# Expert mixtures of a hybrid backbone: gather threaded with the first experts, two more weight buffers, w2 by column halves, paired combines

## The chip, the cores and the metric

One core of a Trainium2 chip runs the whole program. The metric is the time of one execution on the device in microseconds (us); the median of three runs is compared.

## The reference

Four layers work on 256 context and 256 latent tokens of 1024 channels. A layer has a norm, an input projection, three token mixers and an output projection, and then a second norm and a mixture of 16 experts, in which each expert takes the 32 tokens that want it most, separately for context and latent tokens. The change is in the mixture, in the norm at the head of the layer and in the sums of squares between them:

```python
def rmsnorm(x, g):
    y = xf * lax.rsqrt(jnp.mean(xf * xf, axis=-1, keepdims=True) + EPS)
    return (y * g.astype(jnp.float32)).astype(x.dtype)

def modulate(h, shift, scale):
    return h * (1 + scale[:, None]) + shift[:, None]

def moe_ec(h, router_w, w1, w3, w2):
    cap = max(1, CAP_FACTOR * n // N_EXPERTS)          # 32
    probs = jax.nn.softmax((h @ router_w).astype(jnp.float32), axis=-1)
    aff, idx = lax.top_k(jnp.swapaxes(probs, 1, 2), cap)
    xe = h[bidx, idx]
    hid = jax.nn.silu(jnp.einsum('becd,edf->becf', xe, w1)) * jnp.einsum('becd,edf->becf', xe, w3)
    ye = jnp.einsum('becf,efd->becd', hid, w2) * aff[..., None].astype(h.dtype)
    return jnp.zeros_like(h).at[bidx, idx].add(ye)
```

In layers 0 to 2 both streams go through the mixture; in layer 3 only the latent tokens do.

## The kernel before

The residual stream lies transposed in SBUF: `xT` holds 8 blocks of 128 channels by 512 tokens (columns 0 to 255 context, 256 to 511 latent).

**Weights of the experts.** `Weights` (L1474) cuts w1, w3 and w2 of each expert into tiles of 512 KB and loads them, through SP's queue, into a ring of `N_MW` = 22 buffers of the tag `mw`. A pair of experts has 24 tiles in the order w1, w3, w2 (eight each, the two experts in turn), so a mixture has 192. A w1 or w3 tile is 256 input channels by 512 columns (L1490, two runs of 2 KB in each partition), a w2 tile is 128 rows by 1024 columns (L1492, one run of 4 KB). Loads are issued ahead while the output projection runs (`ahead`, two in each of its eight blocks); four of the ring's buffers hold part of that projection's input until its end. After that a load goes out as soon as the tile 22 places before it has been used. SP issues in order.

**Choosing and gathering tokens.** `moe` (L1528) makes the router's softmax, marks the 32 largest of each row with four rounds of max and replace (L1594), numbers the marked tokens by a scan along the row (L1599) and a product (L1601), transposes the numbers (L1604) and compares them with 1 to 32 to get the one-hot matrix `OH` (L1614). The normed tokens are kept as a high and a low part, `tok`. `gather(eh)` (L1622) multiplies them with the one-hot of eight experts, for eight channel blocks `kk` and both streams `s`, and writes `xe`: 16 experts by 64 columns, 32 context tokens and then 32 latent tokens. `gather(0)` stands ahead of all experts, `gather(1)` behind w1 and w3 of pair 0.

**Pairs of experts.** For each of the eight pairs (L1641): w1 and w3 (L1650, the two experts side by side in the array, 64 columns each), the matrix of weights `Ow` and its transpose (L1660 to L1668), the gate (L1670 to L1673), four transposes (L1676), w2 (L1684), whose two column halves are written in turn for each of four row blocks, the scaled outputs as a high and a low part (`yh`, `yl`, L1687, L1688), and the combine (L1694): for each of eight channel blocks two matmuls of 128 x 512 back to token order, added to `xT` by DVE (L1697). The planner of the language orders each engine's instructions by priority and its own estimate of when they are ready; so the trace shows the combine of one pair threaded into w1 of the next.

**Sums and norm.** Behind the last pair, each finished block of `xT` is squared by ACT and summed over its channels by a matmul with ones (`add_all`, L345 to L349): eight in all. Then `rms_scale` (L357) takes the logarithm and the exponential on ACT, and the head of the next layer (L547 to L553) makes the modulated, normed tokens `hh` (high) and `hl` (low) for each of eight blocks: a product on DVE (L549), two scaled shifts on DVE (L552), the high part copied by ACT (L366) and the difference on POOL or DVE in turn (L367). The projection's matmuls (L393) and the small gates (L211) read them.

## Time and profile before

| | us |
|---|---|
| median of 3 runs | 5003.71 (5001.26 to 5008.22) |
| the profiled execution | 5006.14 |
| its span, first to last instruction | 5004.4 |
| PE busy | 4513.4 (90%) |
| DVE busy | 2998.8 (60%) |
| ACT busy | 1470.0 (29%) |
| POOL busy | 1405.1 (28%) |

The mixtures run from about 1027 to 1319, 2296 to 2589, 3573 to 3864 and 4725 to 4988 us of the span; layers 0 to 2 repeat each other closely, so layer 0 stands for them. In the rows below a name such as `L1694` is a line of the kernel before, `out<-in` are the program's tensors (`df`, `dm`, `bi`, `ac`, `ai` are banks of PSUM, `mw` the weight ring), and x counts instructions. fp32 matmuls are two instructions in the trace. PEld is PE's load of the stationary operand. A row of the timeline merges equal instructions that follow one another: its start, the time to the end of the last, and their number. A wait is put down to what came last.

### The profile page before, as it was taken

The numbers are of one execution on the slowest core, as the hardware profiler recorded it, in microseconds if no ns is written. First come the engines' busy times: TensorE is split into PE (matmuls) and PEld (weight loads), VectorE is DVE, ScalarE is ACT, GpSimd is POOL, SyncE is SP. The second block draws the span as 40 slices with busy tenths as digits, with TensorE's granted clock in tenths as the row PEclk, the third lists the DMA queues.
The fourth block names the chain that finished last, engine by engine and source line by source line (L and its number), as shares of the span: only waits on it lengthen the run. The fifth ranks groups of instructions, "written<-read, shape, count | busy, mean of one in ns | idle before, by whom it ended". The sixth has DMA issues, their size and how long they took to land.

```text
span 5004.4 us, 84862 instructions
## 1 busy us (share of the span) xinstructions
PE 4513.4 (90%) x31882; PEld 2934.2 (59%) x31882; DVE 2998.8 (60%) x8123; ACT 1470.0 (29%) x2932; POOL 1405.1 (28%) x1815
## 2 busy tenths in 40 slices
PE   7999999999889999989998999998998888887798
PEld 4666666653466666665336666666633666675533
DVE  4786757533477766663347777656333677776322
ACT  3333323220233332322023333332301433332211
POOL 3332323410243233232014333233300433332400
PEclk9999999999999999999999999999999899898899
DMA  5433446679532434457963244345697233333598
GB/s 219 119 112 110 119 148 202 234 262 393 214 106 65 126 106 125 156 191 257 394 258 110 63 119 112 101 150 167 234 390 289 77 83 84 86 88 107 198 392 315
DMA packets 684010, 886.03 MB, mean 177 GB/s; under 512 B 337072, under 2 KB 361264, under 8 KB 670800
## 3 DMA queue, kind: packets, MB, share of 16 engines
q1 hardware_dynamic: 683600, 880.60, 52.7%
q8 instruction: 252, 4.13, 0.3%
q14 instruction: 158, 1.29, 0.1%
HBM read 795.81 MB, written 84.63 MB: 176 GB/s over the span
## 4 chain that ended last, share of the span: by engine, by line
PE 50%; DVE 20%; DMA 6%; issue 4%; ACT 3%; POOL 2%; SPq 0%; DVEq 0%; ACTq 0%; POOLq 0%
PE df L393 9%; PE dm L393 8%; PE df L1650 5%; PE ai L211 5%; PE bi L211 5%; PE dm L1650 4%; PE bi L1694 3%; PE ac L211 2%; PE ac L1684 2%; PE bi L1684 2%; DMA t<-gates 2%; DVE cv L1037 2%; DMA mw<-in_w_dram 1%; DVE sv L428 1%; POOL wlo L367 1%
## 5 line engine op out<-in xcount | busy, mean ns | idle before, releaser
L367 POOL TENSOR_TENSOR wlo<-wraw,whi 128x512 fp32r<-128x512 f32 x696 | 942.6, 1359 | 1934.3 <-ACT whi L366 1708.0
L393 PE MATMUL df<-big,whi 128*128 128x512 f32 (+1 forms) x2944 | 892.0, 384 | 0.0
L393 PE MATMUL dm<-big,whi 128*128 128x512 f32 (+1 forms) x2368 | 740.1, 392 | 1.1 <-DVE big L367 1.1
L393 PE MATMUL df<-big,wlo 128*128 128x512 f32 (+1 forms) x1536 | 650.8, 424 | 70.3 <-POOL wlo L367 23.2
L366 ACT CAST whi<-wraw 128x512 fp32r<-128x512 f32 x696 | 426.5, 617 | 870.6 <-PE df L393 442.4
L393 PEld LDWEIGHTS df<-big,whi 128*128 128x128 f32 x2944 | 567.5, 201 | 90.8 <-issue 3.7
L393 PE MATMUL dm<-big,wlo 128*128 128x512 f32 (+1 forms) x1248 | 528.5, 424 | 57.0 <-POOL wlo L367 18.6
L393 PEld LDWEIGHTS dm<-big,whi 128*128 128x128 f32 x2368 | 458.9, 198 | 85.4 <-DVE big L367 2.8
L393 PEld LDWEIGHTS df<-big,wlo 128*128 128x128 f32 x1536 | 306.7, 200 | 197.0 <-issue 97.1
L393 PEld LDWEIGHTS dm<-big,wlo 128*128 128x128 f32 x1248 | 247.1, 198 | 164.9 <-issue 71.9
L1650 PE MATMUL df<-mw,big 128*64 128x512 f32 x1024 | 302.2, 610 | 0.0
L1037 DVE SCALAR_TENSOR_TENSOR cv<-cv,par,cv 128x255 f32<-128x255 f32 (+3 forms) x472 | 249.0, 539 | 42.6 <-ACT cv L1034 38.8
L1697 DVE SCALAR_TENSOR_TENSOR big<-bi,der,big 128x256 f32<-128x256 f32 x448 | 191.8, 478 | 120.3 <-PE bi L1694 119.9
L1650 PE MATMUL dm<-mw,big 128*64 128x512 f32 x1024 | 255.7, 594 | 2.1 <-DMA mw<-in_w_dram 1.9
L1657 POOL MEMSET mada<- 128x512 f32 x32 | 16.8, 525 | 800.7 <-PE bi L1694 350.4
L722 DVE SCALAR_TENSOR_TENSOR big<-cv,muc,big 128x252 f32<-128x252 f32 (+2 forms) x280 | 156.6, 581 | 33.2 <-ACT big L719 31.8
L1650 PEld LDWEIGHTS dm<-mw,big 128*64 128x64 f32 x1024 | 80.8, 137 | 152.5 <-issue 136.7
L1688 DVE SCALAR_TENSOR_TENSOR mlof<-ac,aff,mhif 128x512 fp32r<-128x512 f32 x32 | 24.0, 750 | 212.3 <-ACT mhif L1687 212.3
L211 PE MATMUL ai<-AR,BK 64*128 64x128 f32 (+1 forms) x1024 | 124.0, 320 | 29.8 <-POOL BK L905 12.3
L1684 PE MATMUL ac<-mw,mrawf 128*64 128x512 f32 x512 | 139.6, 600 | 9.9 <-ACT mrawf L1678 9.9
L1694 PEld LDWEIGHTS bi<-mada,mhif 128*128 128x128 f32 x256 | 48.0, 187 | 155.1 <-issue 82.7
L1684 PE MATMUL bi<-mw,mrawf 128*64 128x512 f32 x512 | 138.1, 592 | 0.0
(514 smaller groups left out, 7871.8 us busy)
## 6 DMA issues: line engine op xcount, KB each, us to landing
mw<-in_w_dram SPq DMA_DIRECT2D x768, 512.0 KB, 10.4
wraw<-in_w_in_dram SPq DMA_DIRECT2D x536, 256.0 KB, 2.8
adaw<-in_ada_w_dram SPq DMA_DIRECT2D x96, 1024.0 KB, 6.3
gates<-gt SPq DMA_DIRECT2D x114, 256.0 KB, 3.4
wraw<-in_w_branch_dram SPq DMA_DIRECT2D x96, 256.0 KB, 2.7
t<-gates SPq DMA_DIRECT2D x85, 256.0 KB, 3.7
TU<-zoai SPq DMA_DIRECT2D x128, 128.0 KB, 3.1
wraw<-in_w_out_dram SPq DMA_DIRECT2D x64, 256.0 KB, 5.1
```

What stands on the lines that cost most here:

```text
L211: mm(o, a, b, **kw)
L366: se.copy(dst_hi, src)
L367: eng.tensor_tensor(dst_lo, src, dst_hi.bitcast(F32), ALU.subtract)
L393: mm(ps[:, c0:c1], a[:, k % 4, :], bk[:, c0:c1], start=(n == 0), stop=(n == 3 * nk - 1))
L428: ve.tensor_tensor(tv, Xb[:, j + 1:, j:j + 1].to_broadcast(sh), Xb[:, j:j + 1, 0:j].to_broadcast(sh), ALU.mult)
L722: ve.scalar_tensor_tensor(dst, src, muc[:, 1 + q, rb:rb + 1], dst, ALU.mult, ALU.add)
L1037: ve.scalar_tensor_tensor(dst, src, cw[:, cb, t:t + 1], dst, ALU.mult, ALU.add)
L1650: mm(ps[64 * q:64 * q + 64, :], xe[k // 4][:, k % 4, e0 + q, :], wt[q][:, k2 * 512:(k2 + 1) * 512], start=(k == 0), stop=(k == 7))
L1684: mm(py[hf][64 * q:64 * q + 64, :], hT[:, kk, 64 * q:64 * q + 64], wt[q][:, hf * 512:(hf + 1) * 512], start=(kk == 0), stop=(kk == 3))
L1688: ve.scalar_tensor_tensor(yl[hf], py[hf], aff, yh[hf].bitcast(F32), ALU.mult, ALU.subtract)
L1694: mm(pcb[:, n], y[db // 4][:, db % 4 * 128:(db % 4 + 1) * 128], Cm[:, n], start=y is yh, stop=y is yl)
L1697: ve.scalar_tensor_tensor(xT[:, db, cs_], pcb[:, cs_], der[:, 3, db, s:s + 1], xT[:, db, cs_], ALU.mult, ALU.add)
```

## The change

- The ring grows from 22 to 24 buffers (`N_MW`), the cap on loads ahead from 18 to 20 (`N_PRE`; the eight blocks call for 16). Some small tiles of the routing share buffers.
- A w2 tile is now 256 rows by 512 columns, so w2 is multiplied one column half after the other.
- The slots come from a product with a triangular matrix (three small matmuls) in place of scan and product.
- `gather` takes a list of channel blocks. Two blocks are gathered ahead of the experts, then two more ahead of each of the first three steps of pair 0's w1. In every second pair of experts context and latent columns change places.
- Pairs 0 to 5 are combined two by two: the outputs of four experts are masked and added so that one tile holds the context tokens of four experts and another the latent tokens; 32 matmuls of 256 columns then serve two pairs, where 32 of 512 did. Pairs 6 and 7 are combined as before.
- The sums of squares: the squares of blocks 0+1, 2+3 and 4+5 are added on POOL, so five matmuls with ones in place of eight. A dummy logarithm behind the last pair's transposes loads ACT's table early.
- The norm at the layer's head: DVE multiplies by scale and by r in one instruction for each stream, ACT adds the shift while it writes the high part; the low part comes from one DVE instruction per stream (odd blocks) or from another ACT shift and a POOL difference (even blocks).

The diff, cut to its core:

```diff
...
-N_MW = 22
+N_MW = 24
...
-N_PRE = 18
+N_PRE = 20
...
+        def add_two(self, k, x, ps):
+            sq = self.z.mt([512], *(("ys", 2) if k in (1, 3, 5) else ("t2",)))
+            se.activation(sq[:, self.n], x[:, self.n], AF.Square)
+            if k == 0:
+                self.held, self.sent = [], 0
+            if k < 6 and k % 2 == 0:
+                self.first = sq
+            elif k < 6:
+                gp.tensor_tensor(self.first[:, self.n], self.first[:, self.n], sq[:, self.n], ALU.add)
+                self.held.append(self.first)
+            else:
+                self.held.append(sq)
+            while self.held and (k == 7 or k % 2 == 0 and k > 2 and len(self.held) > 1):
+                mm(ps[:, self.n], C["ones"], self.held.pop(0)[:, self.n], start=(self.sent == 0), stop=(self.sent == 4))
+                self.sent += 1
...
                     t = zr.mt([512], "t2")
-                    ve.tensor_tensor(t, xT[:, k, :], r, ALU.mult)
-                    for s in range(2):
-                        ts_ = t[:, s * 256:(s + 1) * 256]
-                        ve.tensor_scalar(ts_, ts_, der[:, 0, k, s:s + 1], mod[:, k, s:s + 1], ALU.mult, ALU.add)
-                    split(hh[:, k, :], hl[:, k, :], t, (gp, ve)[k % 2])
+                    cs_ = [slice(s * 256, s * 256 + 256) for s in range(2)]
+                    for s, c in enumerate(cs_):
+                        ve.scalar_tensor_tensor(t[:, c], xT[:, k, c], der[:, 0, k, s:s + 1], r[:, c], ALU.mult, ALU.mult)
+                    for s, c in enumerate(cs_):
+                        se.activation(hh[:, k, c], t[:, c], AF.Identity, bias=mod[:, k, s:s + 1])
+                    if k % 2:
+                        for s, c in enumerate(cs_):
+                            ve.scalar_tensor_tensor(hl[:, k, c], t[:, c], mod[:, k, s:s + 1], hh[:, k, c].bitcast(F32), ALU.add, ALU.subtract)
+                    else:
+                        for s, c in enumerate(cs_):
+                            se.activation(t[:, c], t[:, c], AF.Identity, bias=mod[:, k, s:s + 1])
+                        gp.tensor_tensor(hl[:, k, :], t, hh[:, k, :].bitcast(F32), ALU.subtract)
...
             else:
-                sy.dma_start(t, A["w2"][l, e, (j - 8) * 128:(j - 7) * 128, :])
+                hf, j = (j - 8) // 2, j % 2
+                src = A["w2"][l, e, j * 256:(j + 1) * 256, hf * 512:(hf + 1) * 512].rearrange("(k p) f -> p k f", p=128)
+                sy.dma_start(t.rearrange("p (k f) -> p k f", k=2), src)
...
-        sel, slot = z.mt([256], "sel"), z.mt([256], "slot")
-        ve.tensor_scalar(sel[lp], wk[lp], -1.0, None, ALU.is_equal)
-        ve.tensor_tensor_scan(slot[lp], C["ones"][lp, 0:1].to_broadcast([64 - 32 * st0, 256]), sel[lp], 0.0, ALU.mult, ALU.add)
-        ve.tensor_tensor(slot[lp], slot[lp], sel[lp], ALU.mult)
+        ve.tensor_scalar(wk[lp], wk[lp], -1.0, None, ALU.is_equal)
         pst = z.psm()
         for q in range(2):
-            te.transpose(pst[:, 64 * q + 32 * st0:64 * q + 64], slot[lp, q * 128:(q + 1) * 128], ident[lp, lp])
-        stm = z.mt([2, 64], "stm")
+            te.transpose(pst[:, 64 * q + 32 * st0:64 * q + 64], wk[lp, q * 128:(q + 1) * 128], ident[lp, lp])
         sv = slice(32 * st0, 64)
-        ve.tensor_copy(stm[:, :, sv], pst[:, 0:128].rearrange("p (q e) -> p q e", q=2)[:, :, sv])
+        sel, stm = z.mt([2, 64], "sel"), z.mt([2, 64], "stm")
+        ve.tensor_copy(sel[:, :, sv], pst[:, 0:128].rearrange("p (q e) -> p q e", q=2)[:, :, sv])
+        pst = z.psm()
+        mm(pst[:, 32 * st0:64], C["mf_0"], sel[:, 0, sv], start=True, stop=True)
+        mm(pst[:, 64 + 32 * st0:128], C["ones"], sel[:, 0, sv], start=True, stop=False)
+        mm(pst[:, 64 + 32 * st0:128], C["mf_0"], sel[:, 1, sv], start=False, stop=True)
+        ve.tensor_tensor(stm[:, :, sv], pst[:, 0:128].rearrange("p (q e) -> p q e", q=2)[:, :, sv], sel[:, :, sv], ALU.mult)
...
+        def gather(eh, kks):
+            for kk in kks:
...
-                    o, pv = xe[g][:, k, 8 * eh:8 * eh + 8, 32 * s:32 * s + 32], ps.rearrange("p (e c) -> p e c", e=8)
+                    xv = xe[g][:, k, 8 * eh:8 * eh + 8, :].rearrange("p (a r q) c -> p a r q c", r=2, q=2)
+                    pv = ps.rearrange("p (a r q c) -> p a r q c", a=2, r=2, q=2)
                     sc, sh = der[:, 1, kk, s:s + 1], mod[:, 24 + kk, s:s + 1]
-                    if s:
-                        se.activation(o, pv, AF.Identity, scale=sc, bias=sh)
-                    else:
-                        ve.tensor_scalar(o, pv, sc, sh, ALU.mult, ALU.add)
-        gather(0)
+                    for r_ in range(2):
+                        o = xv[:, :, r_, :, 32 * (s ^ r_):32 * (s ^ r_) + 32]
+                        if s:
+                            se.activation(o, pv[:, :, r_], AF.Identity, scale=sc, bias=sh)
+                        else:
+                            ve.tensor_scalar(o, pv[:, :, r_], sc, sh, ALU.mult, ALU.add)
+        gather(0, range(2))
...
             for wn in ("w1", "w3"):
                 ps = psd()
                 for kk in range(4):
+                    if pr_ == 0 and wn == "w1" and kk < 3:
+                        gather(0, range(2 * kk + 2, 2 * kk + 4))
                     wt = [W.take() for q in range(2)]
...
                 ab.append(ps)
             if pr_ == 0:
-                gather(1)
...
+                gather(1, range(8))
+            if pr_ < 6 and pr_ % 2 == 0:
...
+                aff, af = z.mt([2], "aff"), z.mt([2, 2], "af", 2)
+                ve.tensor_scalar(Cm[:, n], pc[:, n], 0.0, None, ALU.is_gt)
+                ve.tensor_reduce(aff[:, st0:], pc[:, n].rearrange("p (s w) -> p s w", w=256), AX.X, ALU.add)
+                for r_ in range(2):
+                    for s in range(st0, 2):
+                        ve.tensor_tensor(af[:, r_, s:s + 1], aff[:, s:s + 1], C["qd"][:, r_ ^ s:(r_ ^ s) + 1], ALU.mult)
...
+            if pr_ == 7:
+                se.activation(z.mt([1], "lnt"), hT[:, 0, 0:1], AF.Ln, scale=0.0, bias=C["eps"])
             py = [psum("ac"), psum("bi")]
-            for kk in range(4):
-                wt = [W.take() for q in range(2)]
+            for hf in range(2):
+                for kk in range(4):
+                    if kk % 2 == 0:
+                        wt = [W.take() for q in range(2)]
+                    for q in range(2):
+                        mm(py[hf][64 * q:64 * q + 64, :], hT[:, kk, 64 * q:64 * q + 64], wt[q][:, kk % 2 * 512:kk % 2 * 512 + 512], start=(kk == 0), stop=(kk == 3))
+            r_ = pr_ % 2
+            if pr_ >= 6:
+                yh, yl = [w2k("hif", F32R) for _ in range(2)], [w2k("lof", F32R) for _ in range(2)]
                 for hf in range(2):
-                    for q in range(2):
...
-            yh, yl = [w2k("hif", F32R) for _ in range(2)], [w2k("lof", F32R) for _ in range(2)]
+                    se.activation(yh[hf], py[hf], AF.Copy, scale=aff[:, 0:1])
+                    ve.scalar_tensor_tensor(yl[hf], py[hf], aff[:, 0:1], yh[hf].bitcast(F32), ALU.mult, ALU.subtract)
+                if pr_ == 7:
+                    X["ss"] = psum("dm")
+                for db in range(8):
+                    pcb = psum("bi")
...
+                    if pr_ == 7:
+                        sums.add_two(db, xT[:, db], X["ss"])
+                continue
+            if r_ == 0:
+                ys = [[w2k("rawm") for hf in range(2)], [z.mt([512], "ys", 2) for hf in range(2)]]
...
             for hf in range(2):
-                se.activation(yh[hf], py[hf], AF.Copy, scale=aff)
-                ve.scalar_tensor_tensor(yl[hf], py[hf], aff, yh[hf].bitcast(F32), ALU.mult, ALU.subtract)
-            if pr_ == 7:
-                X["ss"] = psum("dm")
+                for s in range(st0, 2):
+                    if r_ == 0:
+                        se.activation(ys[s][hf], py[hf], AF.Copy, scale=af[:, 0, s:s + 1])
+                    else:
+                        ve.scalar_tensor_tensor(ys[s][hf], py[hf], af[:, 1, s:s + 1], ys[s][hf], ALU.mult, ALU.add)
+            if r_ == 0:
+                continue
+            yh, yl = [[[w2k(x + f, F32R) for _ in range(2)] for f in "fm"] for x in ("hi", "lo")]
+            for hf in range(2):
+                for s in range(st0, 2):
+                    split(yh[s][hf], yl[s][hf], ys[s][hf], (ve, gp)[hf])
             for db in range(8):
                 pcb = psum("bi")
-                for y in (yh, yl):
-                    mm(pcb[:, n], y[db // 4][:, db % 4 * 128:(db % 4 + 1) * 128], Cm[:, n], start=y is yh, stop=y is yl)
+                for s in range(st0, 2):
+                    cs_ = slice(s * 256, (s + 1) * 256)
+                    for y in (yh, yl):
+                        mm(pcb[:, cs_], y[s][db // 4][:, db % 4 * 128:(db % 4 + 1) * 128], Cm[:, cs_], start=y is yh, stop=y is yl)
                 for s in range(st0, 2):
                     cs_ = slice(s * 256, (s + 1) * 256)
                     ve.scalar_tensor_tensor(xT[:, db, cs_], pcb[:, cs_], der[:, 3, db, s:s + 1], xT[:, db, cs_], ALU.mult, ALU.add)
...
```

## Rows read from the trace of the kernel before

**Rows 1.** Stretches: length, busy (count) PE, PEld, DVE, ACT, POOL; clock, DMA share, GB/s

```profile
1044.80:1056.10 11.30, 11.23 (x66) 9.80 (x66) 6.34 (x16) 3.95 (x7) 0.00 (x0) 0.76 0.00 0
1178.70:1210.40 31.70, 29.88 (x120) 10.54 (x120) 11.44 (x26) 2.49 (x6) 0.53 (x1) 1.00 1.04 394
1304.70:1321.30 16.60, 14.47 (x40) 5.85 (x40) 8.18 (x19) 9.64 (x15) 5.08 (x4) 1.00 0.32 91
1327.40:1345.00 17.60, 17.53 (x67) 9.03 (x68) 11.29 (x21) 5.54 (x9) 8.34 (x6) 0.83 0.39 149
4850.00:4950.00 100.00, 93.13 (x396) 34.87 (x393) 24.59 (x52) 9.42 (x15) 1.58 (x3) 1.00 1.04 393
```

**Rows 2.** Waits of weight loads, 1130-1290, then 4800-4972: us, times, longest

```profile
PEld df L1650 <- DMA mw<-in_w_dram: 0.4, 1, 0.4
...
PEld dm L1650 <- DMA mw<-in_w_dram: 13.5, 20, 1.2
```

**Rows 3.** PE in order of time, layer 0: start, us, instruction, count, idle

```profile
1056.14 7.09 PE L1650 MATMUL df<-mw,big 128*64 128x512 f32 x32
...
1178.77 0.49 PE L1694 MATMUL bi<-mada,mhif 128*128 128x512 f32 x1 [0.81 <-ACT mhif L1687]
...
1192.97 7.45 PE L1650 MATMUL dm<-mw,big 128*64 128x512 f32 x31
...
1210.44 0.50 PE L1694 MATMUL bi<-mada,mhif 128*128 128x512 f32 x1 [0.76 <-ACT mhif L1687]
...
1303.62 1.08 PE L1684 MATMUL bi<-mw,mrawf 128*64 128x512 f32 x4
```

**Rows 4.** Loads issued by SP in order of time, layer 0

```profile
1058.10 0.80 SPq L1492 DMA_DIRECT2D mw<-in_w_dram  x2
...
1282.10 1.62 SPq L374 DMA_DIRECT2D wraw<-in_w_in_dram  x2
```

**Rows 5.** DMA issues of the page: count, KB each, median us to landing

```profile
mw<-in_w_dram SPq DMA_DIRECT2D x768, 512.0 KB, 10.4
...
t<-gates SPq DMA_DIRECT2D x85, 256.0 KB, 3.7
...
t<-gates SPq DMA_DIRECT2D x23, 128.0 KB, 2.9
```

**Rows 6.** Loads issued by SP in order of time, last layer

```profile
4841.88 9.40 SPq L1490 DMA_DIRECT2D mw<-in_w_dram  x8
...
4852.20 9.91 SPq L1490 DMA_DIRECT2D mw<-in_w_dram  x8
...
4863.02 9.79 SPq L1492 DMA_DIRECT2D mw<-in_w_dram  x8
```

**Rows 7.** All engines in order of time, layer 0, choosing tokens

```profile
1040.43 1.63 DVE L1599 TENSOR_TENSOR_SCAN slot<-cst,sel 64x256 f32<-64x256 f32 x1
...
1042.10 1.30 DVE L1601 TENSOR_TENSOR slot<-slot,sel 64x256 f32<-64x256 f32 x1
...
1044.87 0.58 PE L1630 MATMUL bi<-OH,mhim 128*128 128x256 f32 x1 [0.94 <-DVE OH L1614]
```

**Rows 8.** Waits of SP, 1056 to 1090: us in total, times, longest

```profile
SPq L1490 <- PE df L1650: 10.5, 5, 7.6
```

**Rows 9.** Groups by line in the tail: count, busy us, mean ns, idle before

```profile
L349 PE MATMUL dm<-t,cst 128*128 128x512 f32 x16 | 8.0, 612 | 0.7 <-ACT t L348 0.7
L1697 DVE SCALAR_TENSOR_TENSOR big<-bi,der,big 128x256 f32<-128x256 f32 x16 | 6.8, 478 | 5.7 <-PE bi L1694 5.7
...
L1694 PE MATMUL bi<-mada,mhif 128*128 128x512 f32 x8 | 4.4, 544 | 1.1 <-ACT mhif L1687 0.8 <-DVE big L1697 0.2 <-DVE mlof L1688 0.2
...
L1694 PEld LDWEIGHTS bi<-mada,mlof 128*128 128x128 f32 x8 | 1.5, 188 | 1.2 <-DVE mlof L1688 0.6 <-issue 0.5
```

**Rows 10.** Groups by line in the first norm of layer 1

```profile
L552 DVE TENSOR_SCALAR t<-t,der,mod 128x256 f32<-128x256 f32 x16 | 5.5, 407 | 0.0
L549 DVE TENSOR_TENSOR t<-big,adm 128x512 f32<-128x512 f32 x8 | 5.4, 689 | 5.2 <-POOL big L367 3.5 <-ACT adm L362 1.6
```

More of the change, by code (lines that the diff above doesn't have):

```diff
@@ L1590, in moe @@
                 tok[g, t] = (hi, lo)
[L1591 removed]
+        wk, m8 = z.mt([256], "lT"), z.mt([8], "m8")
         src = pp[:, 0:256]
@@ L1619, in moe @@
             for xg in xe:
-                gp.memset(xg[:, :, :, 0:32], 0.0)
-        def gather(eh):
-            for kk in range(8):
+                for r_ in range(2):
+                    gp.memset(xg.rearrange("p k (a r q) c -> p k a r q c", r=2, q=2)[:, :, :, r_, :, 32 * r_:32 * r_ + 32], 0.0)
+        def gather(eh, kks):
+            for kk in kks:
                 g, k = kk // 4, kk % 4
@@ L1665, in moe @@
-            Cm = w2k("ada", F32R)
-            aff = z.mt([1], "aff", 2)
-            ve.tensor_scalar(Cm[:, n], pc[:, n], 0.0, None, ALU.is_gt)
-            ve.tensor_reduce(aff, pc[:, n], AX.X, ALU.add)
+                gather(1, range(8))
+            if pr_ < 6 and pr_ % 2 == 0:
+                Ow = w2k("ada").rearrange("p (t q r c) -> p t q r c", t=4, q=2, r=2)
+                for t in range(tl, 4):
+                    s = t // 2
+                    ov = OHf[:, t, e0 * 32:e0 * 32 + 128].rearrange("p (r q c) -> p r q c", r=2, q=2)
+                    av = lg[:, t, e0:e0 + 4].rearrange("p (r q) -> p r q", r=2)
+                    for r_ in range(2):
+                        ve.tensor_tensor(Ow[:, t, :, r_ ^ s], ov[:, r_], av[:, r_, :, None].to_broadcast([128, 2, 32]), ALU.mult)
+                pc = z.psm()
+                for t in range(tl, 4):
+                    te.transpose(pc[:, t * 128:(t + 1) * 128], Ow[:, t].rearrange("p q r c -> p (q r c)"), ident)
+                Cm = w2k("ada", F32R)
+                aff, af = z.mt([2], "aff"), z.mt([2, 2], "af", 2)
+                ve.tensor_scalar(Cm[:, n], pc[:, n], 0.0, None, ALU.is_gt)
+                ve.tensor_reduce(aff[:, st0:], pc[:, n].rearrange("p (s w) -> p s w", w=256), AX.X, ALU.add)
+                for r_ in range(2):
+                    for s in range(st0, 2):
+                        ve.tensor_tensor(af[:, r_, s:s + 1], aff[:, s:s + 1], C["qd"][:, r_ ^ s:(r_ ^ s) + 1], ALU.mult)
+            elif pr_ >= 6:
+                Ow = w2k("ada").rearrange("p (t e c) -> p t e c", t=4, e=2)
+                gp.memset(Ow, 0.0)
+                for t in range(tl, 4):
+                    o = 32 * ((t // 2) ^ (pr_ % 2))
+                    ve.tensor_tensor(Ow[:, t, :, o:o + 32], OHf[:, t, e0 * 32:e0 * 32 + 64].rearrange("p (e c) -> p e c", e=2),
+                                     lg[:, t, e0:e0 + 2, None].to_broadcast([128, 2, 32]), ALU.mult)
+                pc = z.psm()
+                for t in range(tl, 4):
+                    te.transpose(pc[:, t * 128:(t + 1) * 128], Ow[:, t].rearrange("p e c -> p (e c)"), ident)
+                Cm = w2k("ada", F32R)
+                aff = z.mt([2], "aff")
+                ve.tensor_scalar(Cm[:, n], pc[:, n], 0.0, None, ALU.is_gt)
+                ve.tensor_reduce(aff[:, 0:1], pc[:, n], AX.X, ALU.add)
```

19 lines of the change are left out of this document (6 added, 13 removed).

## The prediction

> **What bounds the kernel now.** I read the table of stretches first, for the share of the DMA engines and of PE in each stage of an expert mixture. In layer 0 the gather of the tokens (1044.8 to 1056.1) has a DMA share of 0.00: all weight buffers are full and none is free yet. A pair of experts in the middle (1178.7 to 1210.4) has PE busy for 29.88 of 31.7 us and a DMA share of 1.04 at 394 GB/s: both are at their limit. The tail behind the last w2 (1304.7 to 1321.3) has 0.32 again, and the last layer's middle (4850 to 4950) 1.04 with PE at 93 of 100 [rows 1]. Then the waits of PE's weight loads tell which of the two is late: from 1130 to 1290 they waited 0.4 us for a weight tile, in the last layer 13.5 us in 20 waits, at a granted clock of 1.00 [rows 1, 2]. So layers 0 to 2 are set by PE, with the DMA less than 1% behind it, and layer 3 by the DMA.
>
> PE's order in time gives the prices: a pair takes 1210.44 - 1178.77 = 31.67 us; its w1 stage, into which the combine of the pair before is threaded, 1192.97 - 1178.77 = 14.2, while pair 0's w1, with no combine, took 7.09. The last w2 of layer 0 ends at 1303.62 + 1.08 = 1304.7 [rows 3]. In the DMA queue in order of time the first load into a freed buffer goes out at 1058.10, and the first load for the next layer, right behind the last w2 load, at 1282.10 [rows 4]; with 10.4 us to landing [rows 5] the last w2 tile is there at about 1282.1 - 1.3 + 10.4 = 1291.2. PE then ends w2 13.5 us behind the stream. That lag is what the change can win at most if the stream stays as it is.
>
> **The speed of the stream.** In the last layer eight loads are under way at a time (10.4 us to landing are eight times 1.3), so an issue goes out when the load eight places before it lands. The first eight issues of a pair, paced by landings of w2 tiles, take 4852.20 - 4841.88 = 10.32 us, 1.29 each; the next eight, paced by w1 tiles, 4863.02 - 4852.20 = 10.82, 1.35 each [rows 6]. All are 512 KB; a w2 tile is read as rows of 4 KB, the others as rows of 2 KB. The change reads w2 as half rows of 2 KB, so I price it like w1: 0.06 more for each of the 56 w2 tiles behind the first pair, 3.4 us per layer. The Trainium skill, "DMA: Bandwidth & Descriptors", section Specifications, has a DMA at line rate from 512 B up, by which the halves would cost nothing; the rows disagree by 0.06 us, and by the page the sum would be 13.6 us better (a rival below).
>
> **Layers 0 to 2, to the end of w2.** The scan (1.63) and the product (1.30) of the slots go from DVE's chain; three small matmuls and a product read from PSUM come in. From the scan's start to the first gather matmul there are 1044.87 - 1040.43 = 4.4 us [rows 7]; of these 2.9 go, and about 1.3 come (my estimate: the transposes, the copy and the handing over that stand behind the product now take 4.4 - 2.9 = 1.5 together with the one-hot; between 0.5 and 2), so the gather starts 1.6 earlier. Experts inside the gather: the first slots come free some 6 us earlier, but PE has the same gathers, w1 and w3 to do before it reaches pair 0's w2. The queue runs dry there already today: its longest wait for a free slot is 7.6 us [rows 8], which ends only when w2 frees slots. With two more buffers it is tile 40 of 192 instead of tile 38 that waits for the first w2 slot. So the lead of the stream is 1.6 + 2 x 1.29 = 4.2, less 3.4 for the half rows: 0.8 us, and the last tile lands at 1290.4. Its matmuls are a quarter of a stage, 7.09 / 4 = 1.8 us [rows 3]: end of w2 at 1292.2 by the DMA.
>
> By PE alone: combines threaded into a w1 go from seven to four (pairs 0+1, 2+3, 4+5, then 6), so 3 x 7.1 = 21.3 us go, and 1.6 from the start: 1281.8. A combine of four experts has the same columns in twice as many matmuls; between nothing and 16 more weight loads of 0.19 [rows 9] each, 3.0, three times: 1281.8 to 1290.8. More DVE and ACT work comes (masking, four evictions and four splits every second pair), off the path: in a pair DVE was busy 11.44 and ACT 2.49 of 31.7 [rows 1]. So PE ends before the DMA either way, and the stream sets the end: 1304.7 - 1292.2 = 12.5 gained. Next late is the DMA, in all four layers.
>
> **The tail.** PE is busy 14.47 of 16.6 us from 1304.7 on [rows 1]; 8.0 of it are the sums of squares, eight of two matmuls each, of which five stay: 3.0 gone. PE waits 1.1 for the first evictions [rows 9]; with w2 by halves of its columns the first half is evicted under the second: that goes too. The POOL adds (three of about 1.3, like the four that make up POOL's 5.08 of 16.6 [rows 1]) go under POOL's idle time, and the last two squares need none. Bounds: 2, if the order of PE's queue stays as poor, to 7, where DVE's 16 updates (6.8) [rows 9] with a square and two sums after them are all that is left. I take 4.1. The early load of the logarithm's table is worth nothing here: today's load lies beside the last sums.
>
> **The first norm.** DVE's part falls from 8 x 0.689 + 16 x 0.407 plus the four differences to 24 pieces of about 0.48; ACT gets 24 half pieces for 8 whole ones [rows 9, 10]. DVE's stage would be a third shorter. But from 1327.4 to 1345 PE is busy 17.53 of 17.6 us, at clock 0.83 [rows 1]: it is fed fast enough. Only the first piece comes sooner: 0.69 + 2 x 0.41 and ACT's copy become two halves of 0.48 with ACT's first half under DVE's second, about 0.7 less; with a little of the slow clock, 1. Bounds -1 (ACT late) to 4.
>
> **Sum.** Layers 0 to 2: 3 x (12.5 + 4.1 + 1) = 52.8. Last layer: already paced by the DMA, so its lead of 0.8, and 3 in its tail (sums of half the width, 1.3; evictions 1.1; some of the table load, which is not covered there): 3.8. First norm of layer 0: 1. Together 57.6 us. The profiled execution took 5006.1 (span 5004.4), 2.4 over the median of 5003.7: 5006.1 - 57.6 = 4948.5, or 4946 beside the median.
>
> **Rivals.** *Half rows cost nothing* (they read like 4 KB rows): 3.4 more in each layer, 4932. For it: neighbouring halves are read soon after each other. Against: w1's price. 12%. By the page named above this would be the case. *PE stays the bound*: the wide combine, its splits or the two banks it shares keep PE near its old pace, and w2 ends only 4 us sooner: 3 x (4 + 4.1 + 1) + 4.8 = 32, 4972. For it: twice as many matmuls, and four evictions and four splits that must end before the first of them. 17%. *The order doesn't come as written* (the planner that orders PE's queue keeps the gather whole and the tail as it is): the DMA limit barely moves, the tail gives 2, 3 x (12 + 2) + 3 = 45, 4959. 15%. *The tail and the norm give all they can*: 3 x (12.5 + 7 + 4) + 6 = 76, 4928. 8%. *Slower*: half rows in steps of 4 KB may read worse than whole rows of 2 KB. The nearest rows are the loads of the gates: halves of rows, 128 KB, took 2.9 us where whole rows, 256 KB, took 3.7 [rows 5], 1.57 times the time per byte, though much of that is latency. At 1.29 x 1.57 = 2.03 us a tile the 224 w2 tiles of four layers cost 0.68 x 224 = 152 more: 5098. It turns the result from 1.35 + 57.6 / 224 = 1.61 us a tile on. 8%. *No change*, by smaller losses of the same kind: 4%.
>
> **How the numbers follow.** The forecast has 36%: 4946. Two in ten may be left out: the slower case with no change, and the outer ends of the fast one; the range goes from 4908 (the two fast rivals together, and a little) to 4986 (PE the bound with a tail of nothing). Faster by over 0.2%, about what a measurement of this kernel can tell from no change, holds the forecast and four rivals: 0.88; same 0.04; slower 0.08.
>
> **What would show it.** Right: in layers 0 to 2 PE's loads wait for weight tiles as in the last layer now; 24 loads take 32.4 us instead of 31.9; the last w2 matmuls end 2 us behind the last landing; DMA share stays over 1 to the end. Wrong: w2 tiles that land at 1.29, or above 1.6; PE still without waits for tiles in pairs 5 to 7; a clock below 1.00 between pairs; a tail of 16 us.

## The result and the profile after

The changed kernel takes 4942.2 us (median of four runs, 4935.1 to 4953.0) beside 5005.8 us (5001.3 to 5008.2): a ratio of 0.9876, 95% interval 0.9855 to 0.9897. The forecast was 4946. The profiled execution took 4935.1 us, its span 4933.3, so 71.1 us less than the span of before, of which some 7 are this execution's own (4942.2 - 4935.1).

The total came out as forecast, its parts did not. I measure with two marks in each layer: the start of the softmax's reduction to the maximum on DVE, and the end of the last update of xT behind the mixture. From the first to the second (a mixture) before took 286.0, 287.8, 285.3 and 259.5 us in the four layers, after 276.0, 275.2, 275.3 and 260.8: 31.3 us less where the sum of the prediction had 53.6, and the last layer longer. The stretches between the mixtures are 39.4 us shorter in these two executions, where it had 4 (the first norm).

The stretches of the changed kernel, as in [rows 1] (length; busy us and count of PE, PEld, DVE, ACT, POOL; clock, DMA share, GB/s): pair 5 of layer 0, the tail from the end of w2 to the norm's first product, the first norm of layer 1, the middle of the last layer. Pairs are counted from 0.

```profile
1184.70:1217.20 32.50, 28.52 (x103) 8.75 (x101) 5.46 (x9) 3.68 (x6) 0.00 (x0) 1.00 1.05 387
1288.10:1302.80 14.70, 11.43 (x28) 3.77 (x27) 6.52 (x23) 8.35 (x14) 6.68 (x6) 0.88 0.53 198
1302.80:1318.50 15.70, 11.78 (x43) 4.24 (x44) 13.30 (x24) 10.02 (x24) 5.39 (x4) 0.78 0.40 138
4780.00:4880.00 100.00, 89.78 (x347) 29.38 (x345) 17.57 (x36) 7.46 (x12) 3.59 (x4) 1.00 1.05 387
```

The loads that SP issues, layer 0 and then the last layer, in order of time (start, us of the group, engine, line, count); L1519 loads w2, L1515 w1 and w3:

```profile
1195.02 9.86 SPq L1519 DMA_DIRECT2D mw<-in_w_dram  x8
1205.86 20.72 SPq L1515 DMA_DIRECT2D mw<-in_w_dram  x16
1227.55 9.81 SPq L1519 DMA_DIRECT2D mw<-in_w_dram  x8
1238.35 21.00 SPq L1515 DMA_DIRECT2D mw<-in_w_dram  x16
1260.18 10.00 SPq L1519 DMA_DIRECT2D mw<-in_w_dram  x8
...
4855.27 9.94 SPq L1519 DMA_DIRECT2D mw<-in_w_dram  x8
4866.09 20.79 SPq L1515 DMA_DIRECT2D mw<-in_w_dram  x16
```

In layer 0 the queue now keeps the even step that only the last layer had in [rows 6]: 24 loads take 1227.55 - 1195.02 = 32.5 us. The sixteen issues from 4866.09 on are paced by eight landings of w2 and eight of w1, 1.35 us each (the next w2 load goes out at 4887.75); the w2 step was 1.29 in [rows 6]. The rate is 387 GB/s for 394.

What PE's weight loads waited for from 1100 to 1290 us (us in total, times, longest), which was 0.4 us for weight tiles in [rows 2]:

```profile
PEld dm L1686 <- DMA mw<-in_w_dram: 5.8, 8, 1.2
PEld df L1686 <- DMA mw<-in_w_dram: 5.4, 8, 1.2
```

Of these 11.2 us, 10.6 lie in w1 and w3 of pair 5 (1184.7 to 1206.4); behind them PE waits for no tile. The last w2 load went out at 1269.66; with 10.8 us to landing it is there at 1280.5. PE in order of time shows that w2 ended at 1286.00 + 1.93 = 1287.9, 7.4 us behind it. Between its matmuls (L1745) stands the combine (L1757).

```profile
1276.05 3.65 PE L1745 MATMUL ac<-mw,mrawf 128*64 128x512 f32 x16 [0.67 <-ACT mrawf L1735]
1279.54 1.02 PE L1745 MATMUL bi<-mw,mrawf 128*64 128x512 f32 x2
1280.49 0.50 PE L1757 MATMUL bi<-mada,mhif 128*128 128x512 f32 x1
1281.28 0.50 PE L1757 MATMUL bi<-mada,mlof 128*128 128x512 f32 x1 [0.28 <-DVE mlof L1751]
1281.71 1.93 PE L1745 MATMUL bi<-mw,mrawf 128*64 128x512 f32 x6
...
1286.00 1.93 PE L1745 MATMUL bi<-mw,mrawf 128*64 128x512 f32 x6
```

So two questions went to the chip: which edit shortened the stretches between the mixtures, and why PE is late again at the end of a mixture that the stream sets in its middle.

### The profile page after: what moved, and what is told of

The parts are those of the page before. It is cut to its first block, busy times and chain, and to the rows that moved or that the text cites. A ratio compares the mean times of both kernels' runs of the same rounds, so it can differ in the third digit from the quotient of the medians.

```text
span 4933.3 us, 84704 instructions
## 1 busy us (share of the span) xinstructions
PE 4447.4 (90%) x31792; PEld 2903.0 (59%) x31792; DVE 2927.6 (59%) x8016; ACT 1526.7 (31%) x3100; POOL 1416.8 (29%) x1826
## 3 DMA queue, kind: packets, MB, share of 16 engines
q14 instruction: 158, 1.29, 0.1%
## 5 line engine op out<-in xcount | busy, mean ns | idle before, releaser
L411 PE MATMUL df<-big,whi 128*128 128x512 f32 (+1 forms) x2944 | 884.8, 382 | 0.0
L411 PE MATMUL dm<-big,whi 128*128 128x512 f32 (+1 forms) x2368 | 735.3, 390 | 0.0
L411 PE MATMUL df<-big,wlo 128*128 128x512 f32 (+1 forms) x1536 | 645.9, 420 | 65.9 <-ACT gt L590 21.4
L411 PEld LDWEIGHTS df<-big,whi 128*128 128x128 f32 x2944 | 562.4, 199 | 89.8 <-issue 3.8
L411 PE MATMUL dm<-big,wlo 128*128 128x512 f32 (+1 forms) x1248 | 524.8, 421 | 60.2 <-POOL wlo L385 17.4
L411 PEld LDWEIGHTS dm<-big,whi 128*128 128x128 f32 x2368 | 456.3, 197 | 80.1 <-issue 1.6
L411 PEld LDWEIGHTS df<-big,wlo 128*128 128x128 f32 x1536 | 303.9, 198 | 188.1 <-issue 102.0
L411 PEld LDWEIGHTS dm<-big,wlo 128*128 128x128 f32 x1248 | 245.5, 197 | 163.3 <-issue 57.6
L1686 PE MATMUL df<-mw,big 128*64 128x512 f32 x1024 | 282.8, 604 | 3.7 <-DMA mw<-in_w_dram 3.6
L1728 DVE SCALAR_TENSOR_TENSOR t<-t,df 128x512 f32<-128x512 f32 x32 | 22.0, 687 | 274.1 <-ACT t L1727 274.1
L385 POOL TENSOR_TENSOR mlof<-mrawm,mhif 128x512 fp32r<-128x512 f32 x9 | 11.6, 1284 | 540.3 <-ACT mhif L384 540.3
L1745 PE MATMUL bi<-mw,mrawf 128*64 128x512 f32 x512 | 154.5, 601 | 0.3 <-DMA mw<-in_w_dram 0.3
L1686 PEld LDWEIGHTS df<-mw,big 128*64 128x64 f32 x1024 | 73.3, 136 | 131.4 <-issue 96.1
L1730 DVE TENSOR_TENSOR t<-t,dm 128x512 f32<-128x512 f32 x32 | 22.0, 687 | 193.6 <-PE dm L1686 193.6
L212 PEld LDWEIGHTS ai<-AR,BK 64*128 64x128 f32 x1024 | 91.2, 201 | 72.3 <-issue 30.3
## 6 DMA issues: line engine op xcount, KB each, us to landing
mw<-in_w_dram SPq DMA_DIRECT2D x768, 512.0 KB, 10.8
```

The costliest lines, as they stand in the source:

```text
L212: mm(o, a, b, **kw)
L385: eng.tensor_tensor(dst_lo, src, dst_hi.bitcast(F32), ALU.subtract)
L411: mm(ps[:, c0:c1], a[:, k % 4, :], bk[:, c0:c1], start=(n == 0), stop=(n == 3 * nk - 1))
L1686: mm(ps[64 * q:64 * q + 64, :], xe[k // 4][:, k % 4, e0 + q, :], wt[q][:, k2 * 512:(k2 + 1) * 512], start=(k == 0), stop=(k == 7))
L1728: ve.scalar_tensor_tensor(th, th, 1.0, ab[0], ALU.add, ALU.mult)
L1730: ve.tensor_tensor(hid, th, ab[1], ALU.mult)
```

## The experiments

All twelve runs in one table. "Mixtures" is the sum over the four layers as above, to the last update; "to the norm" adds the time from the last update to the first product of the next norm, for three layers (4.8 us each before); "norm" is the sum over the layers from that product to the end of the norm's 32-matmul product (tile bi<-big,TU); "rest" is the sum from there to the next softmax. The last four columns are one profiled execution, in us; the ratio is to the kernel before on the same chip.

| kernel | median | ratio, 95% interval | mixtures | to the norm | norm | rest |
|---|---|---|---|---|---|---|
| before | 5005.8 | 1 | 1118.6 | 1133.0 | 83.7 | 3725.4 |
| after | 4942.2 | 0.9876 (0.9855-0.9897) | 1087.3 | 1101.7 | 65.9 | 3705.2 |
| n1, before with the new norm | 4984.2 | 0.9954 (0.9936-0.9972) | 1118.9 | 1133.3 | 64.1 | 3726.3 |
| n2, after with the old norm | 4974.5 | 0.9945 (0.9926-0.9965) | 1086.1 | 1100.5 | 87.8 | 3718.7 |
| n3, after, w2 by 4 KB rows | 4938.8 | 0.9876 (0.9856-0.9897) | 1078.5 | 1092.8 | 65.9 | 3718.5 |
| n4, before, w2 by half rows | 5006.5 | 1.0008 (0.9998-1.0018) | 1125.0 | 1139.3 | 83.7 | 3721.4 |
| n5, after with 22 buffers | 4951.3 | 0.9905 (0.9878-0.9931) | 1095.2 | 1109.6 | 65.8 | 3702.5 |
| n6, after, gather first | 4940.1 | 0.9880 (0.9855-0.9906) | 1084.8 | 1099.2 | 65.9 | 3713.4 |
| n7, after, unpaired | 4993.8 | 0.9995 (0.9980-1.0009) | 1130.3 | 1146.5 | 64.2 | 3733.6 |
| n8, after with the scan | 4951.1 | 0.9902 (0.9881-0.9924) | 1084.8 | 1099.2 | 65.9 | 3733.0 |
| n9, after with eight sums | 4954.3 | 0.9910 (0.9889-0.9931) | 1086.6 | 1102.8 | 63.2 | 3724.5 |
| n10, halves in pair 7 alone | 4922.2 | 0.9846 (0.9820-0.9871) | 1064.9 | 1079.2 | 65.9 | 3713.3 |
| n11, no halves | 4929.6 | 0.9854 (0.9833-0.9874) | 1057.3 | 1079.8 | 64.3 | 3727.8 |
| n12, banks exchanged | 4958.2 | 0.9919 (0.9899-0.9939) | 1083.8 | 1104.9 | 64.2 | 3736.4 |

The rest is code that no edit touches, and it goes from 3702 to 3736 us. Two things go with that. One is the granted clock: the four kernels whose profiled execution had a mean clock of 0.946 or 0.948 (n12, before, n7, n11) took 3725 to 3736 us, the three with 0.954 (after, n2, n5) 3702 to 3719. The other is the order in which the planner set this code. In layers 1 and 2 DVE's instructions stand in nearly one order in before, n1, n4 and n12, in another in n7 and n11, and in a third in after and the other seven; the rest of these two layers takes 1920 to 1933 us in the first order, 1921 and 1935 in the second, 1909 to 1922 in the third. What the clock and what the order is worth no run separates. The mixtures, whose pairs of experts run at a clock of 1.00, repeat to 1 or 2 us in a layer, so edits are read from the columns of the stages, and the medians only have to agree.

### The first norm

n1 puts the hunk of the norm into the kernel before, n2 takes it out of the changed one:

```diff
-    ve.tensor_tensor(t, xT[:, k, :], r, ALU.mult)
-    ... scale and shift of both halves on VectorE, then split
+    ve.scalar_tensor_tensor(t[:, c], xT[:, k, c], der[...], r[:, c], ALU.mult, ALU.mult)
+    se.activation(hh[:, k, c], t[:, c], AF.Identity, bias=mod[:, k, s:s + 1])
...
```

Expected of n1:

> The kernel before with the new first norm alone. The prediction (PE is fed fast enough, only the first piece counts) expects 1 us per layer, 4 us: 5002 us beside 5006. The theory from the two traces: the stretches from the last update of a mixture to the next mixture together were 39.3 us shorter after the change (11.1, 7.1, 11.5 and 9.6 us), and the norm is the only edit in them, so the norm alone brings 39 us: 4967 us. Rival: only the norm's own stage is shorter by its cause (about 4 us in a layer, 16 us) and the rest of the 39 us is another order of the queues that came with the other edits: 4990 us.

Expected of n2:

> The changed kernel with the old first norm. By the prediction 4 us are lost: 4946 us. By the theory from the traces 39 us are lost: 4981 us, and the stretches between the mixtures are as long as before. By the rival some 16 us are lost: 4958 us.

n1 brought 19 us in the medians (by its ratio 23, interval 14 to 32), n2 lost 32. In the stages the norm took 22.3, 19.8, 19.8 and 21.8 us before and 15.8, 15.8, 15.8 and 16.6 in n1: 19.6 us, and nothing else moved (mixtures 1118.9, rest 3726.3). n2 differs from after by 21.9 us in the norm and 13.5 in the rest. So the rival holds: about 20 us are the norm's, five in a layer; of the 39.4 us between the two first profiles some 18 are the norm, 20.2 the rest (3725.4 - 3705.2). Of these 20.2, 12.3 lie in layers 1 and 2, whose order changed, and the order came with the other edits, as the rival has it: n1 keeps that of before, n2 that of after. What the 20.2 us owe to the order and what to chance stays open; eight kernels of one order spread from 3702 to 3733 us.

Why the norm could gain, the trace shows. PE of the kernel before in layer 1 in order of time (L393 is the projection w_in, L211 the product with TU), then DVE's last difference there:

```profile
1333.02 2.16 PE L211 MATMUL bi<-big,TU 128*32 128x512 f32 x16
1335.11 0.50 PE L393 MATMUL dm<-big,wlo 128*128 128x512 f32 x1
...
1341.34 0.62 PE L393 MATMUL df<-big,whi 128*128 128x512 f32 x2
...
1342.59 1.27 PE L211 MATMUL bi<-big,TU 128*32 128x512 f32 x8
```

```profile
1341.52 1.24 DVE L367 TENSOR_TENSOR big<-t,big 128x512 fp32r<-128x512 f32 x1 [0.69 <-ACT big L366]
```

The same of the changed kernel:

```profile
1308.76 4.79 PE L212 MATMUL bi<-big,TU 128*32 128x512 f32 x22
1314.37 2.57 PE L212 MATMUL bi<-big,TU 128*32 128x512 f32 x8 [0.82 <-DVE big L574]
...
1318.46 1.04 PE L212 MATMUL bi<-big,TU 128*32 128x512 f32 x2
```

PE was busy all the time before, but with w_in matmuls that stood ready (L393, 31 of them between DVE's first product and the end of the TU product); the eight matmuls that close that product start at 1342.59, as DVE's last difference ends (1342.76). With the new norm 13 of the ready matmuls fall into the stretch (L411), and the product ends at 1319.5, 16.7 us behind the first piece for 19.8. The busy share by itself shows little: of the 3.9 us that PE is idle in the 15.7 above, 3.1 lie ahead of its first norm matmul, at 1305.90. In n1 the last two matmuls of the product wait for DVE's last difference:

```profile
1330.81 1.04 PE L211 MATMUL bi<-big,TU 128*32 128x512 f32 x2 [0.64 <-DVE big L556]
```

### What half rows cost

n3 gives the changed kernel whole rows, n4 the kernel before half rows; the matmuls and the code's order stay, so in both w2 is multiplied with parts of the tiles that are not meant for it. The edit of n3:

```diff
-    src = A["w2"][l, e, j * 256:(j + 1) * 256, hf * 512:(hf + 1) * 512].rearrange("(k p) f -> p k f", p=128)
-    sy.dma_start(t.rearrange("p (k f) -> p k f", k=2), src)
+    sy.dma_start(t, A["w2"][l, e, (j - 8) * 128:(j - 7) * 128, :])
```

Expected of n3:

> The changed kernel, with each w2 tile loaded as 128 whole rows of 4 KB instead of 256 half rows of 2 KB, everything else as it is (the halves of the tiles are then not the weights that the matmuls want: w2 is computed with others). In the trace after the change a tile of half rows took 1.353 us, in the trace of before a tile of whole rows 1.282 us: 0.07 a tile, 4 us for 56 tiles. The prediction, in which the stream sets the end of all four mixtures, expects 13.6 to 16 us: about 4927 us. The theory from the traces: in layers 0 to 2 PE ends w2 8 us behind the last landing without having waited for its tiles, so the stream is worth less than 1 us there and only the last layer gains its 4 to 5 us: about 4936 us. If half rows cost nothing by themselves and the later landings have another cause: 4942 us.

Expected of n4:

> The kernel before, with each w2 tile loaded as 256 half rows of 2 KB, everything else as it is (the matmuls of w2 so use other weights). By the prediction's price of 0.06 us a tile the stream is 3.4 us longer in a layer. In layers 0 to 2 PE is 13.5 us behind the stream and hides it, the last layer shows it: 3.4 to 4 us, 5010 us. If PE's lag hides nothing, because each pair waits for its own tiles, 14 to 16 us: 5021 us. If half rows cost nothing: 5006 us.

n3's mixtures are 1.4, 2.1, 1.3 and 4.0 us shorter than after's: only the last layer is set by the stream to its end. n4's are 1.3, -0.3, 1.0 and 4.4 us longer than before's: PE's lag of 13.5 us hides the price in three layers. Both last layers fit the price of 0.07 us a tile (56 tiles, 3.9 us), and n3 speaks against a stream that sets the end of all four mixtures after the change.

### Buffers and gather

n5 sets `N_MW = 22`, `N_PRE = 18`; n6 has `gather(0, range(8))` ahead of the experts and none inside w1.

Expected of n5:

> The changed kernel with 22 buffers (18 loaded ahead) instead of 24 (20). By the prediction the stream sets the end of all four mixtures and two tiles of lead are 2 x 1.29 = 2.6 us in each: 10 us lost, 4952 us, mixtures of 1087.3 + 10 = 1097 us in the profiled run. By the theory from the traces (PE 8 us behind the stream at the end of layers 0 to 2) less than 1 us is lost there and 2.6 us in the last layer: 4946 us, mixtures of 1091 us.

Expected of n6:

> The changed kernel with the first gather whole ahead of the experts, as in the kernel before. The prediction counts nothing for the threading (PE has the same gathers, w1 and w3 to do before it reaches the w2 of pair 0): 4942 us, mixtures of 1087 us. Rival: the threading fills waits of PE for the evictions of the gather, and the first freed buffers come earlier and carry the stream: 2 us or more in each layer, 4950 us, mixtures of 1095 us, the first freed load later by some 5 us.

n5 lost 1.7, 2.1, 1.4 and 2.8 us in the mixtures, 7.9 in all, nearer to the prediction's 10 than to the theory's 4: a lead counts for most of its worth even where PE is last, since pair 5 waits for its tiles and PE falls behind only after that. n6 lost nothing (2.5 us shorter, within what such sums repeat to): the threading of the experts into the gather is worth nothing here, as predicted.

### Pairing, halves and the end of a mixture

n7 combines every pair for itself; n10 takes halves in pair 7 alone and reads and multiplies w2 by quarters elsewhere; n11 does so in all pairs; n12 exchanges two banks.

```diff
 n7
-            if pr_ < 6 and pr_ % 2 == 0:
+            if False:
...
-            elif pr_ >= 6:
+            else:
...
 n10 (n11: without the condition)
+            if pr_ < 7:
+                for kk in range(4):
+                    wt = [W.take() for q in range(2)]
+                    for hf in range(2):
...
 n12
-            py = [psum("ac"), psum("bi")]
+            py = [psum("bi"), psum("ac")]
```

Expected of n7:

> The changed kernel with every pair combined for itself (as pairs 6 and 7 are), so seven combines of two experts instead of three of four and two of two. By the prediction PE alone ends w2 then 21.3 - 12.5 = 9 us or more later than now and is the bound again: 9 to 12.5 us in each of layers 0 to 2, about 4975 us. By the theory from the traces (a pair of PE takes 31.7 us with its own combine and a pair of the stream now 32.5 us, and PE is 8 us behind anyhow) the pairing is worth at most 5 us a layer: 4957 us. If the combine of two was hidden by the slower stream altogether: 4942 us.

n7's mixtures are 43 us longer than after's (13.6, 14.4, 14.1 and 1.0), longer even than before's. Its stretches, from the start of one w1 to that of the next:

```profile
1169.80:1203.40 33.60, 32.00 (x122) 10.66 (x121) 11.43 (x26) 2.64 (x5) 0.53 (x1) 1.00 1.05 387
1203.40:1236.90 33.50, 31.89 (x122) 10.63 (x121) 11.43 (x26) 2.56 (x5) 0.53 (x1) 1.00 1.05 386
```

A pair is 33.5 us, with as many matmuls as the pair of 31.7 in [rows 1] (122 and 120 records), of which PE was busy 31.9 for 29.9. The stream (32.5) is no longer the bound, PE is. The theory that the pairing was worth 5 us is wrong because it took PE's pair at 31.7: by halves of w2's columns the same work costs PE 1.8 us more. PE in n7, pair 5, shows where: the combine starts under the second half of w2, and its matmuls (hi and lo in turn, a channel block at a time) are set between groups of two and six matmuls.

```profile
1227.82 1.02 PE L1745 MATMUL bi<-mw,mrawf 128*64 128x512 f32 x2
1228.85 0.50 PE L1757 MATMUL bi<-mada,mhif 128*128 128x512 f32 x1
1229.64 0.49 PE L1757 MATMUL bi<-mada,mlof 128*128 128x512 f32 x1 [0.28 <-DVE mlof L1751]
1230.06 1.93 PE L1745 MATMUL bi<-mw,mrawf 128*64 128x512 f32 x6
...
1238.18 0.50 PE L1757 MATMUL bi<-mada,mhif 128*128 128x512 f32 x1 [0.23 <-DVE mlof L1751]
```

From its start at 1224.33 to the next w1 at 1236.87 w2 takes 12.5 us, 5.4 more than the 7.1 of 32 matmuls without a combine, for four of the eight channel blocks; before, all eight cost 7.1 in a w1 [rows 3].

The trace also shows what the price is. The two experts of a pair stand side by side in the array, and where nothing parts them their matmuls start within 10 ns of each other, two every 0.43 us. A combine matmul set between the two parts them, and each expert then takes its 0.43 us alone. So a group of two takes as long as one of four, as in w1 of the kernel before:

```profile
1212.77 1.08 PE L1650 MATMUL df<-mw,big 128*64 128x512 f32 x4
...
1214.44 1.07 PE L1650 MATMUL df<-mw,big 128*64 128x512 f32 x2
```

Of the 96 weight matmuls of such a pair 8 run alone in the kernel before and 16 in n7, the eight more all in the second half of w2. At 0.22 us lost by each they make 1.7 us of the 1.8.

Expected of n10:

> The changed kernel with w2 read and multiplied by halves of its columns in pair 7 alone, and by whole rows, quarter by quarter, in pairs 0 to 6 (as in the kernel before). The stream is 48 x 0.07 = 3.4 us shorter in each layer. By the prediction (the stream sets the end in all four layers) 13.6 us are won: 4928 us. By the theory from the traces the last layer wins 3.4 us and layers 0 to 2 some 1.5 us each, as in the run with whole rows: 4934 us, mixtures of 1079 us. Rival: in pairs 1, 3 and 5 the halves let the combine begin under the second half of w2, and without that PE loses more than the stream gives: 4945 us or more.

Expected of n11:

> The changed kernel with w2 by whole rows, quarter by quarter, in all pairs, the last too. Beside the run with halves in pair 7 alone (mixtures of 1064.9 us) this tells what the halves are worth in the tail. By the prediction 1.1 us of eviction waits in each layer, less 0.07 x 8 for the rows: mixtures of 1067 us. Rival: the halves let half of the last combine with its updates run under w2, and the tail is 4 to 5 us longer without them: mixtures of 1083 us, and nothing is left of the gain over the changed kernel.

n10's mixtures are 6.7, 5.8, 6.3 and 3.7 us shorter than after's. The rows explain 1.3 to 2.1 of that in layers 0 to 2 (n3); the other 4 to 5 us are the order of w2's matmuls. In the changed kernel w2 has eight parted matmuls in each of the pairs 3, 5 and 6 that n10 multiplies by quarters, 1.7 us in each. PE of n10 in pairs 5 and 6 (L1690 is w1 and w3, L1749 w2):

```profile
1200.97 2.43 PE L1690 MATMUL dm<-mw,big 128*64 128x512 f32 x8 [0.28 <-DMA mw<-in_w_dram]
1203.68 1.93 PE L1690 MATMUL dm<-mw,big 128*64 128x512 f32 x6 [0.28 <-DMA mw<-in_w_dram]
...
1214.83 1.02 PE L1749 MATMUL bi<-mw,mrawf 128*64 128x512 f32 x2
...
1246.62 1.41 PE L1749 MATMUL bi<-mw,mrawf 128*64 128x512 f32 x3
```

PE waits for tiles in pair 5, and w2 ends at 1215.9 and 1248.0. The last w2 loads of these pairs go out at 1203.7 and 1235.9, so with 10.5 us to landing PE is 1.7 and 1.6 us behind the stream: what the prediction wanted of the last pair. In the changed kernel it is 2.1 in pair 4, and then 5.4, 6.7 and 7.4 in pairs 5 to 7, each with a part of a combine under its w2: at 33.8 and 33.4 us from one end of w2 to the next against the stream's 32.5 PE can't come back. (In pair 3, too, it is 5.6; PE won that back in pair 4, which has no combine under its w2 and takes 28.2 us.)

n11 has the same time to the norm as n10, 1079.8 for 1079.2: its last w2 ends sooner (245.5 us behind the first gather matmul for 249.2 in layer 0, some 1.6 us behind the last landing), its tail and the way to the norm are longer (9.8 and 9.9 us for 8.6 and 4.8). The halves in the last pair move work from the tail under w2, and here that wins nothing. Part of n11's longer way is another order: in layers 0 and 1 ACT has a cast for the next layer ahead of its last squares, and waits for its load, which it does not in n10:

```profile
1292.40 0.62 ACT L384 CAST whi<-wraw 128x512 fp32r<-128x512 f32 x1 [3.69 <-DMA wraw<-in_w_in_dram]
```

So what the halves are worth there without such a wait, no run shows.

Expected of n12:

> The changed kernel with the PSUM banks of the two halves of w2 exchanged: the first half accumulates in one of the two banks that the combine uses as well, the second half in the bank of its own, so that both banks of the combine are free under the second half. Theory: the halves cost PE time in layers 0 to 2 (unpaired, 33.5 us for a pair where the order by quarters took 31.7) since the combine under the second half has one bank alone and each of its pieces waits for the update of the one before: mixtures of 1087.3 - 3 x 3 = 1078 us or less. Rival: the price is that of going to and fro between w2 and the combine, whatever the bank: 1087 us.

n12's mixtures are 3.5 us shorter to the last update, and to the norm 3.3 longer: the bank is not the cause, and the rival stands. It fits the parted matmuls, of which w2 keeps eight in pairs 3, 5 and 7 and six in pair 6. n12's median is 16.0 us above after's, clear of its interval; by the stages that lies in the rest (3736.4), which has the order of the kernel before.

n10 is the best of the runs: 4922.2 us, a ratio of 0.9846 for 0.9876. The intervals of the two overlap, so the medians alone don't settle it; the 22.4 us in the mixtures do not depend on the rest.

### Counting slots and sums

n8 has the scan and the product again, n9 the eight sums of two matmuls (`add_all`).

Expected of n8:

> The changed kernel with the slots counted by the scan and the product on the VectorE again, ahead of the transposes, in place of the three small matmuls. By the prediction the gather starts 1.6 us later in each layer: mixtures 5 to 6 us longer in the profiled run (1087.3 + 6 = 1093 us), 0.12% of the time. By the theory from the traces (the first gather matmul came 11.7, 11.5, 11.8 and 10.8 us behind the softmax's start after the change, 11.6, 12.8, 11.7 and 10.2 before) the counting on PE is worth nothing: mixtures of 1087 us.

Expected of n9:

> The changed kernel with eight sums of squares of two matmuls each at the end of a mixture, as in the kernel before, in place of the five of paired squares. By the prediction 3.0 us of PE come back in each tail, 11 to 12 us in all: mixtures up to the last update hardly longer, the stretches between the mixtures 3 us longer each, 0.24% of the time. Rival: with half of the last combine now under w2, PE waits in the tail for the updates anyhow, and the eight sums lie in those waits: less than 1 us in a layer.

In n8 the first gather matmul came 2.0, 1.7 and 1.1 us later behind the softmax in layers 0 to 2 and 0.6 sooner in the last, so the three matmuls do start the gather sooner; but the mixtures are not longer (1084.8), and the last w2 load goes out within 0.7 us of after's: the start of the gather sets nothing. n9 lost 1.1 us in all to the norm, not 11, as its rival has it; that the ones-matmuls lie in PE's waits for the updates is an argument from the trace. Both medians are 9 to 12 us above after's; the stages put that into the rest (3733.0 and 3724.5), at the same order as after's, not into the edits.

## Why the prediction was right, and where it was wrong

That the time was right is luck: the sum had 22 us too much in mixtures and tails (53.6 for 31.3) and some 14 too little in the norm (4 for 18), and 13 us of the medians' 63.6 lie in the rest, for which it had no term (63.6 less 31.3 and 18 to 20). 57.6 - 22 + 14 + 13 is 62.6.

**The stream: right but for its lead.** Half rows cost 0.07 a tile (0.06 foreseen), 24 loads take 32.5 us (32.4), and pair 5 waits for tiles. The rival that half rows cost nothing falls by n3 and n4: rows of 2 KB came at 387 GB/s, a mix with a third of 4 KB rows at 394. The Trainium skill, "DMA: Bandwidth & Descriptors", section Specifications, has line rate from 512 B up; in this kernel the measurement differs and decides. The lead was to be 0.8 us: from the first token transposes (1027.1 and 1016.0) the last w2 load went out 253.7 us later before (1280.8) and 253.7 after (1269.66): 0.0 in layer 0. Counted from the softmax it went out 0.1 sooner in layer 1 and 3.3 later in layer 2. The buffers gave their 2.6 or nearly (n5); the 1.6 of the gather's start gave nothing (n8).

**"PE ends before the DMA either way": wrong.** This is the step that failed. I took 21.3 us off PE for the pairing and at most 9 back, and gave the halves a price on the DMA alone. They have one on PE: a combine matmul between the two experts of w2 parts them (n7, n10), and w2 with 7 to 9 such matmuls in it takes 12 us. So w2 ended 7.4 us behind the last landing instead of 1.8, and by 5.6, 6.0 and 3.2 us sooner behind the softmax in layers 0 to 2 where 12.5 were forecast. The wide combine itself was priced well: whole in a w1 (n10, pair 4) it makes that stage 8.9 us longer, for 7.1 and up to 3.0 more. Of the rivals, that PE stays the bound came nearest for layers 0 to 2, by another mechanism than the one I gave it. Without the halves, and without their price on the stream (n11), the mixtures to the norm are 53.2 us shorter than before.

**The tail: wrong in its cause, and too small.** From the end of w2 to the norm's first product it went from 19.4, 20.0 and 20.1 us to 14.9 (1287.9 to 1302.8), 13.3 and 13.5 in layers 0 to 2: 4.5, 6.7 and 6.6 for 4.1. But the term behind 3.0 of it, three of eight sums, is worth 0.4 (n9). Most of the time went because half of the last combine had moved under w2, which is that much longer: with it there the stretch takes 13.3, 13.3 and 12.6 us (n10), without it 19.6, 16.9 and 15.6 (n11, its waits for a load included).

**The last layer: wrong by 5.** 3.8 us were to be won, 1.3 were lost in the mixture and 0.4 won behind it. The half rows cost 4.4 (n4) and the buffers gave 2.8 (n5): counted from the softmax, the last w2 load went out 1.1 us later. Here, too, the halves had a price on PE that the sum lacked: w2 ended 16.4 us behind that load for 12.1, and the tail behind w2 won 4.0 back.

**The first norm: wrong.** The step was that PE, busy 17.53 of 17.6 us [rows 1], was fed fast enough. It was busy in part with work that could stand elsewhere: 31 w_in matmuls lay in the stretch before and 13 after. The Trainium skill, "Perfetto Trace Analysis", section Identifying the Most-Contended Engine, warns that the busy share of matmuls is no good measure of how near PE is to its limit and names the rate of arithmetic and the share of the weight loads instead; the trace agrees, with 9.03 of 17.6 us of weight loads in that row, but the wait of the last product (n1) shows it without a rule. DVE's stage was the bound: it went from 18.7 us (1324.08 to 1342.76) to 13.7 (1302.83 to 1316.52) in layer 1, 27% where I had worked out a third and set it aside, and the product behind it followed, 19.8 to 16.7 us there, 22.3 to 15.8 in layer 0. The wait of DVE for POOL in [rows 10], 3.5 us, belonged to it. Which part of the norm's edit gave how much of that, no run separates.

**The gather with experts inside** was counted at nothing and is worth nothing (n6).

## What to carry to other kernels

An engine that is busy all the time bounds a stage only if the instructions it is busy with are those that the next stage waits for: look for the last of these and at what it waited for. An edit that lets work start earlier under another stage has a price on the engine that both share, here because it parted matmuls that ran side by side; where that engine is within a few per cent of the bound, the price decides. An edit in one stage can change the order of code that it does not touch. When a total comes out right, compare it stage by stage all the same.

## What the hardware showed that was not expected

Two stretches in which the norm is the only edit of the code, from the last update of layer 0 to the softmax of layer 1. The third number from the end is the clock:

```profile
1318.80:2301.20 982.40, 904.82 (x6963) 649.49 (x6960) 662.50 (x1835) 329.79 (x664) 335.52 (x434) 0.96 0.43 134
```

```profile
1298.10:2272.80 974.70, 899.43 (x6966) 643.28 (x6964) 667.42 (x1828) 334.09 (x678) 332.44 (x435) 0.97 0.44 136
```

The first is before, the second after. With nearly the same instructions (6963 and 6966 matmul records) the mean granted clock is 0.96 and 0.97, most of the time at the upper of the two levels (2.4 GHz) and the rest at the lower. The order of the queues differs as well. Over fourteen profiled kernels the rest of the layers differs by 34 us, 0.7% of the time: as much as half of this change. A difference of 10 us between two kernels here is read from a stage at a steady clock, or not at all.
